# The products over partitions of a stick-breaking attention kept in a PSUM bank, and the results of the feed-forward's inner units put first

## The chip, the cores and the metric

The kernel runs on one core of a Trainium2 chip. A core has a matrix engine (PE), a vector engine (DVE), a scalar engine (ACT), a general engine (POOL) and a queue engine (SP) that mostly starts transfers. Each works through its own instructions in a fixed order and waits at semaphores for the others. SBUF is the working memory; PSUM holds eight banks of 128 partitions by 512 float32, into which PE writes and which DVE and ACT can read and write. POOL touches SBUF alone. The metric is the time of one execution on the device, in microseconds, lower being better.

## The reference

One layer of a hybrid encoder over a sequence of 2048 positions with 1024 channels, in float32. After an RMS norm, one projection feeds three mixers; their results are joined, projected back and added, and a squared-ReLU feed-forward follows.

```python
h = _rmsnorm(x, g_attn); p = h @ w_in            # 2816 columns
y_a = a_b * causal_conv3(a_c * a_h)
g = causal_conv31(b0 * sigmoid(b1)) + b_conv_b   # 256 channels
y_b = silu(_layernorm(g, ln_b_g, ln_b_b))
# y_c: stick-breaking attention, 8 heads of 64
z = q @ k.T * scale
log_beta = log_sigmoid(z)
log_1m = where(s < t, log_beta - z, 0)
suffix = reverse_cumsum(log_1m) - log_1m
a = where(s < t, exp(log_beta + suffix), 0)
o = a @ v
x = x + concat([y_a, y_b, y_c]) @ w_out
h2 = _rmsnorm(x, g_ffn)
x = x + square(relu(h2 @ w_ff1)) @ w_ff2         # 4096 inner units
return _rmsnorm(x, g_final)
```

The attention has no softmax: the weight of key s for query t is sigmoid(z) there, times the product of sigmoid(-z) over all keys between s and t. That running product over keys is what the changed code works out.

## The kernel before

Activations lie transposed, channels on partitions and 512 positions along a row, so the sequence makes four blocks (tb 0 to 3). Each float32 product is computed as three matmuls over a high and a low half of the operands (`mm3`, lines 103, 105 and 107, which is why most PE instructions carry these lines). The splitting into halves is `split` (L88 on ACT, L90 on DVE or POOL).

**Two large stages.** In the first, `p_half(0)` and `p_half(1)` compute the input projection of two blocks each. Beside them run the convolution mixer (`mixer_b`), the splitting of weights, and, in the second half, the attention of the first block. In the second stage, `block(tb)` computes for each of the four blocks the output projection, the 32 inner units `ffn1(c)` and, for each group of four of them, the second product `ffn2(g)`; beside blocks 0 to 2 runs the attention of blocks 1 to 3.

**The order of the work.** Work that runs beside the main line is a Python generator that yields a cost now and then. `weave(main, sides)` advances each side in proportion to the main line: an entry `(side, cost, t0, t1, last)` means that the side has come through `cost` units when the main line goes from t0 to t1. This gives the program order. A planner then simulates the engines with a cost model and writes each engine's instructions down in the order in which they came up there; among those that are ready it takes the earlier in program order, and what stands in `tc.high_priority(offset=HP)` is taken as 200 instructions earlier. On the chip each engine keeps this written order: if the next one has to wait, all behind it on that engine wait too.

**PSUM banks** are shared out by tags. In the second stage: three for the projections (`d`, also of the inner units `ps_u` and results `ps_y`), three for logits (`z`), one each for `ps_q` and `ps_o`. In the first stage: three `d`, one `c` for the convolution mixer, two `z`, one each for `q` and `o`.

**The attention** of one head and block. `a_pass1` (L542) makes logits per group of keys (`a_z`: matmuls L518 and L519 into a `z` bank), then two sigmoids on ACT: sigmoid(z) goes to the tile `A`, sigmoid(-z) to `om` (three diagonal groups, `a_diag`, L532 and L533) or back into the bank (L600). DVE multiplies up sigmoid(-z) over the groups in a tile `R` (L603), POOL multiplies `A` by it (L601). Keys are dealt out so that each partition holds a run of keys; what is left is the product over partitions. For this, DVE turns blocks of 32 by 32 around (L564 and L581 for the diagonal, 256 columns each, L609 for earlier keys, 512 columns) into a tile `T` of 16 segments of 33. Column 32 of each segment is set to 0 by POOL (L563, L608). `a_cross_a` (L612) then runs a scan backwards over the 528 columns (L617), where the tile `d1` (0, and 1 at each segment's end) restarts the product. Four groups of 32 partitions remain; their products go through a small tile `C` of 128 by 16 in SBUF: the last quarter is set to 1 (POOL, L620) or copied from `tot` (L622), three small multiplies go from quarter to quarter (L625), for the diagonal a fourth makes `tot` (L629), and one multiply applies `C` to `T` (L631). `a_pass2` turns the result back into the bank `ps_q` (L649), multiplies the `A` tiles by it (L652, L659), splits them (L88 on ACT and L90 on POOL, `Ahi` and `Alo`) and multiplies with the values (L697, L705, L706 into `ps_o`). With 8 heads and 4 blocks there are 32 products of the diagonal kind and 24 of the other, 56 in all.

**The feed-forward.** `ffn1(c)` runs 24 matmuls into a bank `ps_u`, then ACT squares the positive part in place (L917, L918) and copies it as the high half `fh` (L926), and DVE makes the low half `fl` (L927). `ffn2` runs 12 matmuls per output tile into `ps_y`, and DVE adds them to `acc` (L952). Since the norm's factor comes after the squaring, `acc` is multiplied by `ms` after the third inner unit: a small matmul spreads it into a `z` bank (L973, `spread`, L134), ACT copies it to SBUF, DVE multiplies the eight tiles (L975).

**The convolution mixer** (`mixer_b`, L441): per block and half of the channels 31 taps on DVE (L450, L452) into the bank `ps_c`, a copy by ACT (L456), a mean over channels on PE (L459), squares on ACT (L464), their sum on POOL (L467) and a column sum on PE (L127), a root on POOL (L118), and the normalised output.

Of the kernel before, what the change touches and what calls it, by code (L numbers as in the profile page):

```python
# [7 lines left out]
F32 = mybir.dt.float32  # L8
# [7 lines left out]
P = 128  # L16
# [18 lines left out]
def f(ap):  # L35
    return ap.bitcast(F32)
# [32 lines left out]
class Trunk:  # L69
# [126 lines left out]
    def attention_consts(self, ctx):  # L196
        nc = self.nc
        c = ctx.enter_context(self.tc.tile_pool(name="aconsts", bufs=1))
        self.d1 = c.tile([P, 16, 33], F32, name="d1")
        nc.vector.memset(self.d1, 0.0)  # L200
        nc.vector.memset(self.d1[:, :, 32:33], 1.0)
# [239 lines left out]
    def mixer_b(self, hf):  # L441
        nc = self.nc
        for tb in (2 * hf, 2 * hf + 1):
            acc = []
            for c in range(2):
# [10 lines left out]
                nc.scalar.activation(acc[c], t, AF.Copy)  # L456
            mean = self.psum("ps_mean", "c")
# [9 lines left out]
            nc.gpsimd.tensor_tensor(sqs[0], sqs[0], sqs[1], op=ALU.add)  # L467
            yv = self.rsqrt(self.colsum(sqs[:1], "c"), 1.0 / 256.0, LN_EPS)
# [73 lines left out]
    def a_pass1(self, g):  # L542
# [18 lines left out]
        nc.vector.tensor_tensor(om[:, hi2], om[:, lo], om[:, hi2], op=ALU.mult)  # L561
        T = pool.tile([P, 16, 33], F32, name="T", tag="T1", bufs=ab["T1"])
        nc.gpsimd.memset(T[:, :, 32:33], 0.0)  # L563
        nc.vector.transpose(T[:, 0:8, 0:32], om[:, hi2])  # L564
# [7 lines left out]
        R = new("R", ab["R"])  # L572
# [7 lines left out]
        nc.vector.tensor_tensor(om[:, hi2], om[:, hi2], R[:, hi2], op=ALU.mult)  # L580
        nc.vector.transpose(T[:, 8:16, 0:32], om[:, hi2])  # L581
        A0.append(t)
        yield 1
        tot = self.a_cross_a(g, T, None)
# [22 lines left out]
        T = pool.tile([P, 16, 33], F32, name="T", tag="T2", bufs=1)  # L607
        nc.gpsimd.memset(T[:, :, 32:33], 0.0)  # L608
        nc.vector.transpose(T[:, :, 0:32], R)  # L609
        self.a_cross_a(g, T, tot)  # L610

    def a_cross_a(self, g, T, seed):  # L612


        nc = self.nc
        fl = lambda x: x.rearrange("p a b -> p (a b)")[:, ::-1]
        nc.vector.tensor_tensor_scan(fl(T), fl(T), fl(self.d1), 1.0, op0=ALU.mult, op1=ALU.add)  # L617
        C = self.tiny.tile([P, 16], F32, name="C", tag="C", bufs=3)
        if seed is None:
            nc.gpsimd.memset(C[96:128], 1.0)  # L620
        else:
            nc.vector.tensor_copy(C[96:128], seed)  # L622
        for a in (2, 1, 0):
            s, d = slice(32 * a + 32, 32 * a + 64), slice(32 * a, 32 * a + 32)
            nc.vector.tensor_tensor(C[d], C[s], T[s, :, 0], op=ALU.mult)  # L625
        tot = None
        if seed is None:
            tot = self.tiny.tile([32, 16], F32, name="tot", tag="tot", bufs=2)
            nc.vector.tensor_tensor(tot, C[0:32], T[0:32, :, 0], op=ALU.mult)  # L629
        qt = T[:, :, 1:33]  # L630
        nc.vector.tensor_tensor(qt, qt, C.unsqueeze(2).to_broadcast([P, 16, 32]), op=ALU.mult)  # L631
        g["qd" if seed is None else "ql"] = qt
        return tot
# [190 lines left out]
    def block(self, tb, before):  # L824
# [76 lines left out]
        def ffn1(*cs):  # L901
# [14 lines left out]
            for c, ps in zip(cs, pus):  # L916
                nc.scalar.activation(ps, ps, AF.Relu)  # L917
                nc.scalar.activation(ps, ps, AF.Square)  # L918
                if tb == 3 and c > FC - G:

                    hi = self.at.tile([P, TB], F32R, name="fh", tag="Ahi", bufs=self.ab["Ahi"])
                    lo = self.at.tile([P, TB], F32R, name="fl", tag="Alo", bufs=self.ab["Alo"])
                else:
                    hi = hp.tile([P, TB], F32R, name="fh", tag="fh", bufs=G + 1)
                    lo = hp.tile([P, TB], F32R, name="fl", tag="fl", bufs=G + 1)
                nc.scalar.activation(hi, ps, AF.Copy)  # L926
                nc.vector.tensor_tensor(lo, ps, f(hi), op=ALU.subtract)  # L927
                fh[c], fl[c] = hi, lo
            yield 2.6 * len(cs)

        def ffn2(g, cols=slice(0, TB), ahead=0, again=0):
# [13 lines left out]
            for d in range(DC):  # L945
# [6 lines left out]
                nc.vector.tensor_tensor(acc[d][:, cols], acc[d][:, cols], ps, op=ALU.add)  # L952
# [19 lines left out]
        ms = hp.tile([P, TB], F32, name="ms", tag="ss", bufs=2)  # L972
        nc.scalar.activation(ms, self.spread(mt, "z"), AF.Copy)  # L973
        for d in range(DC):
            nc.vector.tensor_tensor(acc[d], acc[d], ms, op=ALU.mult)  # L975
        ss2 = hp.tile([P, TB], F32, name="ss2", tag="ss", bufs=2)
        sq7 = []
        for c in range(3, FC):
            yield from ffn1(c)
            if c < w2b:  # L980
                need2(c)
            if c % G == 0 and not (tb == 3 and c == FC - G):
                yield from ffn2(c // G - 1)
# [41 lines left out]
    def build(self):  # L1025
        tc = self.tc
        with ExitStack() as ctx:
# [6 lines left out]
            with ExitStack() as c1:  # L1034
# [12 lines left out]
                self.ab = dict(Kl=1, A0=6, om=2, R=1, T1=2, Alo=2, Ahi=2, Vl=1, late=1, yc=2)  # L1047
                weave(self.p_half(0), [(Side(self.mixer_b(0)), 83, 20, 225, True), (Side(self.x_norms()), 24, 60, 180, True)])
                self.heads = {}
                a0 = Side(self.attention([(h, 0) for h in range(H)]))  # L1050
                weave(self.p_half(1), [(Side(self.mixer_b(1)), 98, 0, 200, True), (a0, 28, 0, 210, True), (Side(self.pre_split()), len(self.presplit), 0, 200, True)])
            with ExitStack() as c2:
# [7 lines left out]
                self.ab = dict(Kl=1, A0=15, om=2, R=2, T1=1, Alo=3, Ahi=3, Vl=2, late=2, yc=1)  # L1060
# [59 lines left out]
```

## Time and profile before

| | |
|---|---|
| median of 3 runs | 2449.74 us (2442.66 to 2449.86) |
| the profiled execution | 2452.1 us, of which 2450.4 us are its span |
| mean granted PE clock | 0.992 of full speed |
| busy: PE, weight load | 2390.6, 2012.8 us |
| busy: DVE, ACT, POOL | 1620.1, 1040.6, 1161.3 us |
| DMA | 549.06 MB, 224 GB/s over the span |

The median is taken over runs without the profiler; the profile is of one further execution, and every duration below is of that one. "Busy" is the time in which an engine had at least one instruction under way. A row of a group names line, engine, operation, output and inputs, the shapes and the count; then the group's busy time and the mean of one instruction. A row of the waits says that an instruction stood because of another's: time in total, how often, the longest. A row of the windows gives, for a stretch of time, its length and then the busy time of PE, weight load, DVE, ACT and POOL, each with the number of instructions, then the granted clock of PE as a share of full speed, the DMA engines' busy share and GB/s.

### The profile page before, as it was taken

The page shows a single profiled execution, that of the slowest core. Times are in us where ns is not written, and L with a number is a line of the kernel's source. Part 1 is how long each engine was busy: PE and PEld are TensorE (multiplying, and loading weights), DVE is VectorE, ACT ScalarE, POOL GpSimd, SP SyncE. Part 2 cuts the span into 40 slices and gives each one's busy share as a digit, 9 for nine tenths or more (in the row PEclk, how much of TensorE's full clock was granted, in tenths as well). Part 3 has the DMA queues.
Part 4 walks back from the last instruction along what each step waited for, and adds up shares of the span by engine and source line. Part 5 has one row for each costly group of instructions (what it writes and reads, how often), then busy time and mean ns, then how long its engine had stood idle before and what let it go on. Part 6 is the DMA issues. An engine that isn't in the chain of part 4 may idle for free.

```text
span 2450.4 us, 32556 instructions
## 1 busy us (share of the span) xinstructions
PE 2390.6 (98%) x11316; PEld 2012.8 (82%) x11316; DVE 1620.1 (66%) x2380; ACT 1040.6 (42%) x1910; POOL 1161.3 (47%) x1221
## 2 busy tenths in 40 slices
PE   8999998999899999998999999999999999999998
PEld 7889877898788878887888888888888888888887
DVE  7957799943898977857777778577667735212114
ACT  5232532333466556534555555345555532121121
POOL 0342577641676666524676666168878720000000
PEclk9999999999999999999999999999999999999999
DMA  7569976779688777786877776876666556655555
GB/s 260 192 244 350 300 247 219 243 258 273 166 232 238 215 220 199 198 287 225 239 253 230 230 217 213 273 219 186 196 188 190 184 180 209 238 194 188 200 182 190
DMA packets 237061, 549.06 MB, mean 224 GB/s; under 512 B 26720, under 2 KB 100448, under 8 KB 218464
## 3 DMA queue, kind: packets, MB, share of 16 engines
q1 hardware_dynamic: 180304, 480.89, 58.1%
q0 software_dynamic: 37504, 56.64, 10.9%
q10 hardware_dynamic: 19088, 9.44, 1.3%
q8 instruction: 90, 1.47, 0.2%
q14 instruction: 75, 0.61, 0.1%
HBM read 390.38 MB, written 148.11 MB: 220 GB/s over the span
## 4 chain that ended last, share of the span: by engine, by line
PE 76%; DVE 15%; DMA 5%; issue 2%; POOL 1%; ACT 1%; SPq 0%; DVEq 0%; POOLq 0%; ACTq 0%
PE ps_y L107 8%; PE ps_y L103 8%; PE ps_y L105 8%; PE ps_u L103 7%; PE ps_u L105 7%; PE ps_u L107 7%; PE ps_p L105 4%; PE ps_p L107 4%; PE ps_p L103 4%; DVE A L659 2%; PE ps_x L103 2%; PE ps_z L518 2%; PE ps_x L105 2%; PE ps_x L107 2%; PE ps_z L519 2%
## 5 line engine op out<-in xcount | busy, mean ns | idle before, releaser
L90 POOL TENSOR_TENSOR Alo<-A,Ahi 128x512 fp32r<-128x512 f32 x288 | 395.1, 1383 | 104.2 <-PE ps_o L706 52.3
L952 DVE TENSOR_TENSOR acc<-acc,ps_y 128x512 f32<-128x512 f32 (+1 forms) x264 | 175.4, 667 | 195.6 <-PE ps_y L107 193.9
L107 PE MATMUL ps_y<-fl,w 128*128 128x512 f32 (+1 forms) x1056 | 279.8, 385 | 14.7 <-DVE fl L927 14.7
L103 PE MATMUL ps_u<-hh,w 128*128 128x512 f32 x1024 | 279.0, 393 | 6.2 <-DMA w<-s_w 6.2
L103 PE MATMUL ps_y<-fh,w 128*128 128x512 f32 (+1 forms) x1056 | 281.4, 386 | 2.5 <-DVE acc L952 1.3
L105 PE MATMUL ps_y<-fh,w 128*128 128x512 f32 (+1 forms) x1056 | 278.9, 384 | 0.0
L105 PE MATMUL ps_u<-hh,w 128*128 128x512 f32 x1024 | 275.0, 390 | 0.6 <-DVE w L90 0.6
L107 PE MATMUL ps_u<-hl,w 128*128 128x512 f32 x1024 | 275.0, 389 | 0.0
L601 POOL TENSOR_TENSOR A<-A,R 128x512 f32<-128x512 f32 x168 | 227.7, 1357 | 76.7 <-ACT A L599 54.6
L118 POOL TENSOR_TENSOR rs_y<-rs_v,mhalf 128x4 f32<-128x4 f32 (+1 forms) x13 | 14.7, 1131 | 523.3 <-DVE rs_v L117 486.1
L107 PEld LDWEIGHTS ps_y<-fl,w 128*128 128x128 f32 x1056 | 195.8, 189 | 55.9 <-DVE fl L927 17.0
L917 ACT ACTIVATE ps_u<-ps_u 128x512 f32<-128x512 f32 x128 | 74.8, 585 | 378.8 <-PE ps_u L107 378.5
L105 PEld LDWEIGHTS ps_y<-fh,w 128*128 128x128 f32 x1056 | 196.0, 189 | 40.2 <-DMA w<-wraw 0.4
L103 PEld LDWEIGHTS ps_y<-fh,w 128*128 128x128 f32 x1056 | 194.3, 189 | 40.7 <-DVE acc L952 2.1
L88 ACT ACTIVATE Ahi<-A 128x512 fp32r<-128x512 f32 x288 | 177.3, 627 | 118.4 <-PE ps_o L705 58.0
L105 PEld LDWEIGHTS ps_u<-hh,w 128*128 128x128 f32 x1024 | 192.1, 188 | 42.4 <-DVE w L90 1.5
L107 PEld LDWEIGHTS ps_u<-hl,w 128*128 128x128 f32 x1024 | 192.1, 188 | 40.1
L927 DVE TENSOR_TENSOR fl<-ps_u,fh 128x512 fp32r<-128x512 f32 x128 | 87.5, 685 | 207.1 <-ACT fh L926 206.6
L103 PEld LDWEIGHTS ps_u<-hh,w 128*128 128x128 f32 x1024 | 187.4, 189 | 42.5 <-DMA w<-s_w 6.4
L603 DVE TENSOR_TENSOR R<-ps_z,R 128x512 f32<-128x512 f32 x168 | 115.6, 688 | 126.4 <-ACT ps_z L600 93.8
L452 DVE SCALAR_TENSOR_TENSOR ps_c<-g,wb,ps_c 128x512 f32<-128x512 f32 x240 | 179.6, 748 | 4.6
L90 DVE TENSOR_TENSOR w<-wraw,w 128x512 fp32r<-128x512 f32 x152 | 150.4, 1007 | 24.1 <-ACT w L88 23.8
(175 smaller groups left out, 4881.2 us busy)
## 6 DMA issues: line engine op xcount, KB each, us to landing
w<-s_w SPq DMA_DIRECT2D x200, 512.0 KB, 3.4
w<-s_w SPq DMA_DIRECT2D x68, 1024.0 KB, 4.8
wraw<-in_w SPq DMA_DIRECT2D x192, 256.0 KB, 4.7
w<-s_w_out SPq DMA_DIRECT2D x64, 512.0 KB, 5.0
s_w<-w SPq DMA_DIRECT2D x32, 1024.0 KB, 5.4
s_w<-w SPq DMA_DIRECT2D x56, 512.0 KB, 4.4
Qd<-KQ SPq DMA_DIRECT2D x64, 256.0 KB, 6.4
xraw<-in_xT SPq DMA_DIRECT2D x48, 256.0 KB, 5.0
```

The costliest lines, as they stand in the source:

```text
L88: nc.scalar.activation(hi, x, AF.Copy)
L90: e.tensor_tensor(lo, x, f(hi), op=ALU.subtract)
L103: self.nc.tensor.matmul(ps, wh, xh, start=start and k == 0, stop=False)
L105: self.nc.tensor.matmul(ps, wl, xh, start=False, stop=False)
L107: self.nc.tensor.matmul(ps, wh, xl, start=False, stop=stop and k == n - 1)
L452: nc.vector.scalar_tensor_tensor(t, g[:, k : k + TB], self.wb[:, c, k : k + 1], t, op0=ALU.mult, op1=ALU.add)
L518: nc.tensor.matmul(z[:, oc], keys, g["qh"][:, qc], start=k == 0, stop=False)
L601: nc.gpsimd.tensor_tensor(t, t, R, op=ALU.mult)
L603: nc.vector.tensor_tensor(Rn, z, R, op=ALU.mult)
L917: nc.scalar.activation(ps, ps, AF.Relu)
L927: nc.vector.tensor_tensor(lo, ps, f(hi), op=ALU.subtract)
L952: nc.vector.tensor_tensor(acc[d][:, cols], acc[d][:, cols], ps, op=ALU.add)
```

## The change

The 32x32 turns of a head go into a bank of the tag `z` instead of into `T`; for that the diagonal's two halves are first collected in one tile `Rd` (a third user of the tag `R`, now with 2 buffers in both stages). The scan reads this bank and `d1`, without the extra column: `max` with `d1` (1 at each segment's end, 0 elsewhere) takes the place of the multiply-and-add that restarted it. `C` lies in the first 16 columns of the same bank, once the scan has read them. The two memsets are DVE's now: the last quarter of `C`, and a column of ones in `T` after the small multiplies. `T1` has one buffer in both stages.

`ms` stays in the bank that `spread` wrote, without ACT's copy; four of the eight multiplies come before the inner unit 3, four after it. The four instructions behind each inner unit, and the addition in `ffn2`, are put at high priority. `mixer_b` gets five more yields per block (three ahead of the mean, two ahead of the column sum), and its costs in `weave` become 115 (from 83) and 116 (from 98).

```diff
-        self.d1 = c.tile([P, 16, 33], F32, name="d1")
+        self.d1 = c.tile([P, TB], F32, name="d1")
         nc.vector.memset(self.d1, 0.0)
-        nc.vector.memset(self.d1[:, :, 32:33], 1.0)
+        nc.vector.memset(self.d1[:, 31:TB:32], 1.0)
...
                 nc.scalar.activation(acc[c], t, AF.Copy)
+            for _ in range(3):
+                yield 1.8
             mean = self.psum("ps_mean", "c")
...
             nc.gpsimd.tensor_tensor(sqs[0], sqs[0], sqs[1], op=ALU.add)
+            for _ in range(2):
+                yield 1.8
             yv = self.rsqrt(self.colsum(sqs[:1], "c"), 1.0 / 256.0, LN_EPS)
...
-        nc.vector.tensor_tensor(om[:, hi2], om[:, lo], om[:, hi2], op=ALU.mult)
-        T = pool.tile([P, 16, 33], F32, name="T", tag="T1", bufs=ab["T1"])
-        nc.gpsimd.memset(T[:, :, 32:33], 0.0)
-        nc.vector.transpose(T[:, 0:8, 0:32], om[:, hi2])
+        Rd = new("R", 2)
+        nc.vector.tensor_tensor(Rd[:, lo], om[:, lo], om[:, hi2], op=ALU.mult)
...
-        nc.vector.tensor_tensor(om[:, hi2], om[:, hi2], R[:, hi2], op=ALU.mult)
-        nc.vector.transpose(T[:, 8:16, 0:32], om[:, hi2])
+        nc.vector.tensor_tensor(Rd[:, hi2], om[:, hi2], R[:, hi2], op=ALU.mult)
...
-        T = pool.tile([P, 16, 33], F32, name="T", tag="T2", bufs=1)
-        nc.gpsimd.memset(T[:, :, 32:33], 0.0)
-        nc.vector.transpose(T[:, :, 0:32], R)
-        self.a_cross_a(g, T, tot)
+        self.a_cross_a(g, R, tot)
...
+        X = self.ps.tile([P, TB], F32, name="ps_t", tag="z", bufs=self.banks["z"])
+        T = self.at.tile([P, TB + 1], F32, name="T", tag="T1" if seed is None else "T2", bufs=1)
+        nc.vector.transpose(X, R)
-        nc.vector.tensor_tensor_scan(fl(T), fl(T), fl(self.d1), 1.0, op0=ALU.mult, op1=ALU.add)
-        C = self.tiny.tile([P, 16], F32, name="C", tag="C", bufs=3)
+        nc.vector.tensor_tensor_scan(T[:, 0:TB][:, ::-1], self.d1[:, ::-1], X[:, ::-1], 1.0, op0=ALU.max, op1=ALU.mult)
+        C = X[:, 0:16]
         if seed is None:
-            nc.gpsimd.memset(C[96:128], 1.0)
+            nc.vector.memset(C[96:128], 1.0)
...
+        first = T[:, 0:TB:32]
-            nc.vector.tensor_tensor(C[d], C[s], T[s, :, 0], op=ALU.mult)
+            nc.vector.tensor_tensor(C[d], C[s], first[s], op=ALU.mult)
...
-        qt = T[:, :, 1:33]
-        nc.vector.tensor_tensor(qt, qt, C.unsqueeze(2).to_broadcast([P, 16, 32]), op=ALU.mult)
+        nc.vector.memset(T[:, 32 : TB + 1 : 32], 1.0)
+        qt = T[:, 1 : TB + 1]
+        q3 = qt.rearrange("p (a b) -> p a b", a=16)
+        nc.vector.tensor_tensor(q3, q3, C.unsqueeze(2).to_broadcast([P, 16, 32]), op=ALU.mult)
...
-            for c, ps in zip(cs, pus):
-                nc.scalar.activation(ps, ps, AF.Relu)
...
+            with self.tc.high_priority(offset=HP):
+                for c, ps in zip(cs, pus):
+                    nc.scalar.activation(ps, ps, AF.Relu)
...
-                nc.vector.tensor_tensor(acc[d][:, cols], acc[d][:, cols], ps, op=ALU.add)
+                with self.tc.high_priority(offset=HP):
+                    nc.vector.tensor_tensor(acc[d][:, cols], acc[d][:, cols], ps, op=ALU.add)
...
-        ms = hp.tile([P, TB], F32, name="ms", tag="ss", bufs=2)
-        nc.scalar.activation(ms, self.spread(mt, "z"), AF.Copy)
+        ms = self.spread(mt, "z")
         for d in range(DC):
+            if d == DC // 2:
+                yield from ffn1(3)
             nc.vector.tensor_tensor(acc[d], acc[d], ms, op=ALU.mult)
...
-        for c in range(3, FC):
+        for c in range(4, FC):
...
-                weave(self.p_half(0), [(Side(self.mixer_b(0)), 83, 20, 225, True), (Side(self.x_norms()), 24, 60, 180, True)])
+                weave(self.p_half(0), [(Side(self.mixer_b(0)), 115, 20, 225, True), (Side(self.x_norms()), 24, 60, 180, True)])
...
-                weave(self.p_half(1), [(Side(self.mixer_b(1)), 98, 0, 200, True), (a0, 28, 0, 210, True), (Side(self.pre_split()), len(self.presplit), 0, 200, True)])
+                weave(self.p_half(1), [(Side(self.mixer_b(1)), 116, 0, 200, True), (a0, 28, 0, 210, True), (Side(self.pre_split()), len(self.presplit), 0, 200, True)])
```

More of the change, by code (lines that the diff above doesn't have):

```diff
@@ L571, in a_pass1 @@
         nc.gpsimd.tensor_tensor(t[:, hi2], t[:, hi2], om[:, lo], op=ALU.mult)
-        R = new("R", ab["R"])
+        R = new("R", 2)
         nc.vector.tensor_tensor(R[:, lo], om[:, lo], om[:, hi2], op=ALU.mult)
@@ L579, in a_pass1 @@
         nc.gpsimd.tensor_tensor(t, t, R, op=ALU.mult)
[L580 to L581 removed]
+        nc.vector.tensor_tensor(Rd[:, hi2], om[:, hi2], R[:, hi2], op=ALU.mult)
         A0.append(t)
         yield 1
[L584 removed]
+        tot = self.a_cross_a(g, Rd, None)
         if not i:
@@ L1059, in build @@
                 self.kmax = 1536
-                self.ab = dict(Kl=1, A0=15, om=2, R=2, T1=1, Alo=3, Ahi=3, Vl=2, late=2, yc=1)
+                self.ab = dict(Kl=1, A0=15, om=2, Alo=3, Ahi=3, Vl=2, late=2, yc=1)
                 at = Side(self.attention([(h, i) for i in (1, 2, 3) for h in range(H)]))
```

27 lines of the change are left out of this document (13 added, 14 removed).

## The prediction

> **What bounds the kernel now.** I read the page first, for the busy shares of the engines:
>
> ```profile
> span 2450.4 us, 32556 instructions
> ...
> PE 2390.6 (98%) x11316; PEld 2012.8 (82%) x11316; DVE 1620.1 (66%) x2380; ACT 1040.6 (42%) x1910; POOL 1161.3 (47%) x1221
> ```
>
> PE is busy for 2390.6 of 2450.4 us, and the change takes no matmul away. So it can only shorten PE's idle time, 59.8 us, and what PE loses where it runs slowly. The second view is therefore the waits of PE alone, longest first (engine, tile, line, what it waited for; total us, times, longest us):
>
> ```profile
> PE ps_y L107 <- DVE fl L927: 14.7, 6, 7.4
> PE ps_p L311 <- ACT wh L88: 6.5, 1, 6.5
> PE ps_u L103 <- DMA w<-s_w: 6.2, 6, 1.8
> PE ps_z L518 <- ACT A L533: 5.9, 1, 5.9
> PE ps_mean L459 <- ACT cb L456: 4.1, 1, 4.1
> PE ps_ss L127 <- POOL sq L467: 3.1, 1, 3.1
> PE ps_o L697 <- POOL Alo L90: 2.4, 2, 1.9
> PE ps_z L518 <- DVE R L603: 1.7, 2, 1.1
> PE ps_y L103 <- DVE acc L952: 1.3, 2, 1.0
> ```
>
> A few single waits make up most of it. The third view, windows of 10 us behind these waits, shows a second price (length; PE, weight load, DVE, ACT, POOL busy; then PE's granted clock, DMA share, GB/s):
>
> ```profile
> 380.00:390.00 10.00, 10.00 (x42) 7.96 (x41) 9.79 (x11) 1.26 (x2) 6.85 (x8) 0.85 0.93 362
> 390.00:400.00 10.00, 6.93 (x22) 5.52 (x21) 7.93 (x12) 3.83 (x8) 9.98 (x10) 0.66 0.46 136
> 640.00:650.00 10.00, 3.80 (x10) 3.05 (x11) 9.91 (x16) 1.09 (x2) 3.81 (x7) 0.66 0.41 118
> 860.00:870.00 10.00, 8.35 (x28) 6.94 (x29) 7.55 (x12) 2.59 (x6) 5.55 (x7) 0.66 0.36 110
> 1110.00:1120.00 10.00, 4.12 (x12) 2.80 (x11) 9.90 (x11) 4.32 (x9) 7.06 (x9) 0.67 0.71 240
> ```
>
> A granted clock of 0.66 over 10 us is 3.4 us lost. Every wait of 3 us or more inside the run is followed by such a loss, so it costs about double. DVE is nearly full in most of these rows. The timeline (start, length) shows what it did ahead of the longest:
>
> ```profile
> 632.08 12.27 DVE L975 TENSOR_TENSOR acc<-acc,ms 128x512 f32<-128x512 f32 x8
> ...
> 645.47 0.68 DVE L927 TENSOR_TENSOR fl<-ps_u,fh 128x512 fp32r<-128x512 f32 x1
> ```
>
> Eight multiplies by `ms` took 12.27 us, and the low half `fl` that PE needed stood behind them until 645.47. Ahead of the wait near 860, ACT was held too (in brackets its idle time and what ended it):
>
> ```profile
> 857.94 0.60 ACT L532 ACTIVATE om<-ps_z 128x512 f32<-128x512 f32 x1 [2.82 <-DVE T L564]
> ```
>
> **The change part by part: the products.** Why did DVE need so long? The instructions that use `T`, with shortest, median and longest duration in ns:
>
> ```profile
> L625 DVE TENSOR_TENSOR C<-C,T x168: 172/181/4320, 291.7 to 1960.0; 32x16 f32<-32x16 f32 x168
> L617 DVE TENSOR_TENSOR_SCAN T<-T,d x56: 1236/1644/5677, 289.6 to 1955.5; 128x528 f32<-128x528 f32 x56
> L631 DVE TENSOR_TENSOR T<-T,C x56: 671/674/1124, 295.4 to 1960.3; 128x512 f32<-128x512 f32 x56
> L649 DVE STREAM_TRANSPOSE ps_q<-T x56: 704/709/727, 297.3 to 1961.0; 128x512 f32<-128x512 f32 x56
> L564 DVE STREAM_TRANSPOSE T<-om x32: 396/433/447, 273.1 to 1913.3; 128x256 f32<-128x256 f32 x32
> L581 DVE STREAM_TRANSPOSE T<-om x32: 427/445/447, 288.6 to 1915.5; 128x256 f32<-128x256 f32 x32
> ```
>
> A multiply of 32x16 takes 172 ns at best and 4320 at worst. The rows with two inputs in SBUF stretch, L617 and L625 by microseconds and L631 by up to 0.45 us; the turns (L649, L564, L581), with one input, do not. The groups (busy us, mean ns) show the same beside a multiply that reads PSUM, L603:
>
> ```profile
> L452 DVE SCALAR_TENSOR_TENSOR ps_c<-g,wb,ps_c 128x512 f32<-128x512 f32 x240 | 179.6, 748 | 4.6
> ...
> L603 DVE TENSOR_TENSOR R<-ps_z,R 128x512 f32<-128x512 f32 x168 | 115.6, 688 | 126.4 <-ACT ps_z L600 93.8 <-issue 14.3 <-POOL A L601 13.3
> L617 DVE TENSOR_TENSOR_SCAN T<-T,d 128x528 f32<-128x528 f32 x56 | 101.9, 1819 | 1.1
> L625 DVE TENSOR_TENSOR C<-C,T 32x16 f32<-32x16 f32 x168 | 90.0, 536 | 5.6
> ...
> L975 DVE TENSOR_TENSOR acc<-acc,ms 128x512 f32<-128x512 f32 x32 | 33.4, 1109 | 2.6 <-ACT ms L973 2.6
> ```
>
> The change puts one input of L617, L625, L631 and L975 into PSUM. For the scan the floor is 1.236 us times 512/528, 1.20 us, the ceiling today's mean of 1.82; I take 1.20, since L603 at 0.688 shows no surcharge for a bank over L631 at 0.674. So 56 x (1.82 - 1.20) = 35 us of DVE go. The small multiplies: between 0.18 and today's 0.536; I take 0.2, 168 x 0.34 = 56 us. `ms`: 32 x (1.109 - 0.688) = 13 us, and ACT's four copies go, for which DVE waited 2.6 us. The turns: 32 x (0.433 + 0.445 - 0.709) = 5 us. DVE gains two memsets, nearest to this row (same shape, stepped):
>
> ```profile
> L201 DVE MEMSET d<- 128x16 f32 x1 | 0.1, 72 | 0.1
> ```
>
> That is (32 + 56) x 0.072 = 6 us, at most. DVE's sum: 1620 - 35 - 56 - 13 - 5 + 6 = about 1517 us busy. None of this is time of the kernel by itself; it counts where PE waits for DVE.
>
> One rule speaks against `ms` in its bank. The Trainium skill, "VectorE: DVE Perf Modes", section "Rules for kernel authors", advises to copy a matmul's output from PSUM to SBUF first if many operations will use it. By it the eight multiplies would rather get dearer. The rows L603 and L975 disagree: 688 ns from PSUM, 1109 ns on average from SBUF; at best they are equal.
>
> POOL loses 56 + 32 memsets, and with them the waits in its queue (who waited for the instructions on `T`: us, times):
>
> ```profile
>   POOL T L608: 54.2, 22
>   POOL T L563: 45.1, 21
>   ACT om L532: 28.5, 6
> ```
>
> POOL stood 99.3 us with its split `Alo` queued behind, which PE's `ps_o` needs; I count nothing for that, though the 2.4 us row could go. `om` is free one turn earlier, since `Rd` takes its product out; that shortens ACT's 28.5 us.
>
> **What PE gets back**, by edit. High priority puts L917 to L927 ahead of attention work in the written order; no DMA is moved past anything by it. That, with the shorter DVE queue, removes the `fl` waits: 14.7 us, and 3.4 us of clock at 640 and at 860, 21.5 us. What is late next there is `fh` on ACT, ready at about 635 in the first case, two us ahead of PE's need. `ms` from its bank, four and four: the wait for ACT's A at 1110, 5.9 us plus 3.3 us of clock, 9.2 us; DVE was held in it just as at 632. Behind the added inner unit only its weights are asked for, in the same order as before. The yields in `mixer_b`: the mean's 4.1 us, the column sum's 3.1 us, clock 1.5 and 3.4 us, 12.1 us; the three steps, 5.4 of 116 units spread over 200 us, move the matmul 9 us later, the two steps 6 us, more than each wait. L952 at high priority: 1.3 us. Together 44.1 us. Not touched: the first load's 6.5 us, the weight DMAs' 6.2 us, the 1.7 us for R.
>
> At the column sum the wait was only 3.1 us. The Trainium skill, "TensorE: Matmul & The Clock Gate", section "HAM oscillation — how this bites in real kernels", has the rule that idle gaps above about 3.4 us cost clock. By it that wait would have been free of the second price, and the sum 40.7 us. The row 390 to 400 at 0.66 decides for 44.1.
>
> **What it adds for PE.** `X` holds one of three `z` banks (one of two in the first stage) from the turn to the last multiply: 0.709 + 1.20 + 3 x 0.2 + 0.15 + 0.674, 3.3 us if nothing comes between, 56 times; `ms` holds one through a whole inner unit, four times. The next logits on PE wait for that bank, and PE's queue, the feed-forward's matmuls too, stands behind them. DVE's turn itself waits for a free bank, with `fl`, R and `acc` behind it; `Rd` and R now fill both buffers of their tag, so ACT's first R of the earlier keys (L597) waits until POOL and DVE are done with them, with the squarings behind it. No row shows this. The nearest rows from below: L603 releases a `z` bank 168 times and PE lost 1.7 us to it, 0.01 us each. From above: an event like the one at 1110, 9.2 us, at every eighth `X`, 64 us. I take two new events of 3.5 us and 3.4 us of clock, about 14 us: near the lower end, because L603 is the same kind of release, but not nothing, since the planner writes the whole order anew.
>
> The sum on the profiled execution: 2452.1 - 44.1 + 14 = 2422.0 us. That execution lies 2.4 us above the median of the three runs, so 2419.6, rounded to **2420 us**.
>
> **The rivals.**
>
> Half 1 becomes DVE's. Its load there (same columns as the windows above):
>
> ```profile
> 270.00:520.00 250.00, 238.60 (x1153) 199.32 (x1152) 222.43 (x325) 86.67 (x160) 186.14 (x201) 0.97 0.78 255
> ```
>
> DVE is busy 222 of 250 us and full near 390. The 62 taps of a block (62 x 0.748 = 46 us of DVE) were spread over 36/98 of 200 us, 73 us; now 36/116, 62 us: 12 points more load just where the projection's results are taken out. For it: the row 380 to 390. Against it: PE hardly waits for those results now, and the yields leave DVE freer in between. Then the mixer's 12.1 us stay and one more event comes: 44.1 - 12.1 - 14 - 7 = 11 us of gain, 2439 us.
>
> The time stays where it is. The waits are put down to an engine by which semaphore came last; if what stretches is only moved (L580, L578, L573, L561 and the weight split keep two SBUF inputs), the new order makes six events of 7 us elsewhere, 42 us, and about 2450 us results. That is also what comes if the bank doesn't free the scan and the small multiplies from their stretching.
>
> Slower: the `z` banks. The same place as the cost above, at its upper end: 64 us lost, 44.1 won, 2452.1 + 20 - 2.4 = 2470 us. It decides from 44.1/9.2, that is from five such events among 56 products. For it: the wait at 1110 is just this kind, PE's order standing behind a `z` bank. Against it: the stretching that made that event is what the change removes.
>
> Better than forecast: no new event, and the `Alo` wait gone: 2452.1 - 44.1 - 2.4 - 2.4 = 2403 us.
>
> **How the numbers follow.** Forecast (2405 to 2432 us) 0.54; half 1 bound by DVE (2432 to 2442) 0.14; better (below 2405) 0.04; no net change (2442 to 2457) 0.14; slower by the banks (above 2457) 0.14. About 0.3%, 7 us, is what a measurement of this kernel can tell from no change. So faster 0.72, same 0.14, slower 0.14. The range from 2402 to 2453 us takes in the forecast, the first rival, the full gain and most of the unchanged case; it leaves out the slower case and the rest, about 2 in 10.
>
> **What would show it.** In the profile after: L625 and the scan with medians near their minima and no durations of several us, DVE near 1517 us busy; no wait of PE for `fl` above 2 us, none at the mean and the column sum; granted clock at 1.00 from 600 to 1200 us. The forecast is wrong if PE's waits show a `z` matmul behind `X`'s multiply, DVE turns waiting for a bank, or L597 waiting for R; if DVE gets its 100 us and PE's idle time stays near 60 us; or if half-clock windows come back at new places.

## The result and the profile after

The changed kernel takes **2420.49 us** (median of 5 runs, 2415.74 to 2422.02) against 2449.74 us (median of 5, 2442.66 to 2455.13): a ratio of 0.9875, 95% interval 0.9852 to 0.9897. The forecast was 2420. Its profiled execution took 2415.74 us and was the shortest of the five, so the two profiles lie further apart than the medians do, 36.4 us of span against 29.3 us. First its page, the shares of the engines:

```profile
span 2414.0 us, 32476 instructions
...
PE 2379.1 (99%) x11316; PEld 2005.3 (83%) x11316; DVE 1534.0 (64%) x2436; ACT 1043.6 (43%) x1906; POOL 1128.6 (47%) x1133
```

The span is 36.4 us shorter with the same matmuls. PE's idle time fell from 59.8 to 34.9 us, its busy time by 11.5 us; most of that is clock: on work, stretches at half clock cost 13.0 us before and 4.0 us after. DVE lost 86 us where 103 were forecast. Second, PE's waits, the longest first:

```profile
PE ps_p L311 <- ACT wh L88: 6.2, 1, 6.2
PE ps_u L103 <- DMA w<-s_w: 6.1, 6, 1.6
PE ps_z L522 <- DVE T L635: 4.8, 3, 3.4
PE ps_R L134 <- POOL rs_y L118: 2.8, 2, 1.7
PE ps_z L522 <- ACT A L537: 2.7, 1, 2.7
```

The waits for `fl`, at the column sum and for `Alo` are gone, and the mean's, in a row further down, is 0.4 us. New is the third row: a logits matmul that waits for the multiply by `C`, the last reader of `X`. Third, the windows around it and at the places where the clock had been at 0.66:

```profile
320.00:330.00 10.00, 6.65 (x26) 5.30 (x25) 9.77 (x21) 3.27 (x7) 3.35 (x4) 0.83 0.79 288
360.00:370.00 10.00, 7.32 (x30) 5.72 (x29) 9.67 (x16) 2.23 (x4) 6.77 (x7) 0.88 0.88 288
...
640.00:650.00 10.00, 10.00 (x48) 8.34 (x47) 7.74 (x13) 6.80 (x14) 10.00 (x13) 1.00 0.48 115
860.00:870.00 10.00, 10.00 (x46) 8.23 (x45) 4.61 (x8) 5.29 (x10) 5.50 (x6) 1.00 0.81 166
1110.00:1120.00 10.00, 10.00 (x46) 8.49 (x45) 5.90 (x9) 5.72 (x11) 4.72 (x4) 1.00 0.46 165
```

In this execution the second stage holds its full clock. The two losses left stand behind the two waits of logits in the first stage, 1.7 us each (the second low stretch goes on past 370; from 365 to 373 the clock is 0.79). It is not so in every execution: a further kernel with the same written order, `no_hp` below, shows a clock of 0.66 from 1086 to 1091, from 1096 to 1101 and from 2065 to 2070. Fourth, the instructions on the bank `X`, which the trace calls `ps_t` (ns: shortest, median, longest):

```profile
L627 DVE TENSOR_TENSOR ps_t<-ps_t,T x168: 173/181/194, 293.5 to 1922.3; 32x16 f32<-32x16 f32 x168
L616 DVE STREAM_TRANSPOSE ps_t<-R x56: 710/727/729, 288.8 to 1918.9; 128x512 f32<-128x512 f32 x56
L618 DVE TENSOR_TENSOR_SCAN T<-d,ps_t x56: 1194/1212/1222, 290.1 to 1920.4; 128x512 f32<-128x512 f32 x56
L635 DVE TENSOR_TENSOR T<-T,ps_t x56: 672/689/693, 298.0 to 1922.6; 128x512 f32<-128x512 f32 x56
```

None of these instructions stretches any more: the small multiplies end at 194 ns at worst, before at 4320, the scan at 1222, before at 5677.

Where the time went, by stretches that hold the same work. Each begins with the first logits matmul (the second half of the projection) or with the first output-projection matmul of a block. Before:

```profile
268.90:557.40 288.50, 277.10 (x1473) 237.78 (x1473) 234.44 (x346) 99.09 (x183) 190.40 (x205) 0.98 0.77 252
557.40:1038.80 481.40, 467.22 (x2140) 388.86 (x2139) 386.70 (x542) 270.93 (x503) 287.66 (x328) 0.99 0.76 217
1038.80:1536.20 497.40, 485.71 (x2218) 408.33 (x2218) 376.60 (x547) 257.48 (x475) 297.44 (x309) 0.99 0.75 237
1536.20:2039.20 503.00, 497.67 (x2254) 417.56 (x2253) 318.55 (x472) 241.47 (x439) 311.26 (x308) 1.00 0.64 199
```

After:

```profile
270.10:553.10 283.00, 273.00 (x1458) 233.48 (x1457) 228.47 (x352) 96.15 (x180) 179.22 (x188) 0.99 0.79 257
553.10:1018.30 465.20, 462.85 (x2139) 385.67 (x2139) 359.89 (x561) 272.49 (x502) 280.74 (x297) 1.00 0.78 225
1018.30:1508.00 489.70, 484.37 (x2218) 407.07 (x2217) 344.62 (x563) 258.40 (x474) 286.71 (x285) 1.00 0.76 241
1508.00:2003.40 495.40, 494.61 (x2254) 417.41 (x2253) 295.94 (x486) 242.65 (x438) 303.72 (x292) 1.00 0.66 202
```

Second half of the projection: 5.5 us shorter. Block 0: 16.2. Block 1: 7.7. Block 2: 7.6. The first half and block 3 together hardly changed. These are differences of one profile each; a table behind the experiments shows which of them come again.

### The profile page after: what moved, and what is told of

Same layout as the page of the kernel before. It is cut to its first block, busy times and chain, and to the rows that moved or that the text cites. A ratio compares the mean times of both kernels' runs of the same rounds, so it can differ in the third digit from the quotient of the medians.

```text
span 2414.0 us, 32476 instructions
## 1 busy us (share of the span) xinstructions
PE 2379.1 (99%) x11316; PEld 2005.3 (83%) x11316; DVE 1534.0 (64%) x2436; ACT 1043.6 (43%) x1906; POOL 1128.6 (47%) x1133
## 4 chain that ended last, share of the span: by engine, by line
PE 84%; DMA 6%; DVE 6%; issue 1%; ACT 1%; POOL 1%; SPq 1%; POOLq 0%; DVEq 0%; ACTq 0%
PE ps_y L107 9%; PE ps_y L105 9%; PE ps_y L103 9%; PE ps_u L103 9%; PE ps_u L105 9%; PE ps_u L107 9%; PE ps_p L107 4%; PE ps_p L105 4%; PE ps_p L103 3%; PE ps_z L522 2%; PE ps_z L523 2%; PE ps_x L103 2%; PE ps_x L105 2%; PE ps_x L107 2%; PE ps_o L710 2%; PE ps_o L709 2%
## 5 line engine op out<-in xcount | busy, mean ns | idle before, releaser
L90 POOL TENSOR_TENSOR Alo<-A,Ahi 128x512 fp32r<-128x512 f32 x288 | 385.3, 1347 | 147.0 <-ACT Ahi L88 69.9
L103 PE MATMUL ps_u<-hh,w 128*128 128x512 f32 x1024 | 279.4, 392 | 6.4 <-DMA w<-s_w 6.1
L103 PE MATMUL ps_y<-fh,w 128*128 128x512 f32 (+1 forms) x1056 | 281.2, 384 | 0.0
L602 POOL TENSOR_TENSOR A<-A,R 128x512 f32<-128x512 f32 x168 | 222.4, 1326 | 121.7 <-ACT A L600 103.3
L107 PE MATMUL ps_y<-fl,w 128*128 128x512 f32 (+1 forms) x1056 | 278.6, 383 | 0.1
L107 PE MATMUL ps_u<-hl,w 128*128 128x512 f32 x1024 | 275.8, 390 | 0.0
L107 PEld LDWEIGHTS ps_y<-fl,w 128*128 128x128 f32 x1056 | 195.0, 188 | 39.4 <-DVE fl L932 0.6
L107 PEld LDWEIGHTS ps_u<-hl,w 128*128 128x128 f32 x1024 | 192.1, 188 | 40.1
L103 PEld LDWEIGHTS ps_y<-fh,w 128*128 128x128 f32 x1056 | 193.6, 188 | 36.8
L103 PEld LDWEIGHTS ps_u<-hh,w 128*128 128x128 f32 x1024 | 186.9, 188 | 42.4 <-DMA w<-s_w 8.1
```

What stands on the lines that cost most here:

```text
L90: e.tensor_tensor(lo, x, f(hi), op=ALU.subtract)
L103: self.nc.tensor.matmul(ps, wh, xh, start=start and k == 0, stop=False)
L107: self.nc.tensor.matmul(ps, wh, xl, start=False, stop=stop and k == n - 1)
L602: nc.gpsimd.tensor_tensor(t, t, R, op=ALU.mult)
```

## The experiments

Twelve kernels, in three sets of four. Each set has its own runs of the kernel before beside it; only ratios to those are compared. The first set leaves out one part of the change, the second makes one part alone, the third takes parts asunder.

### Leaving out high priority

```diff
-            with self.tc.high_priority(offset=HP):
-                for c, ps in zip(cs, pus):
-                    nc.scalar.activation(ps, ps, AF.Relu)
+            for c, ps in zip(cs, pus):
+                nc.scalar.activation(ps, ps, AF.Relu)
...
-                with self.tc.high_priority(offset=HP):
-                    nc.vector.tensor_tensor(acc[d][:, cols], acc[d][:, cols], ps, op=ALU.add)
+                nc.vector.tensor_tensor(acc[d][:, cols], acc[d][:, cols], ps, op=ALU.add)
```

> The changed kernel without high priority for the four instructions behind an inner unit and for the addition in ffn2; all else changed. The changed kernel took 2420.5 us, the one before 2449.7. Theory: the written order made the low half fl late, so waits of PE for fl come back, at least two of over 3 us with the half clock behind them: 2430 to 2442 us. Rival: what made fl late was the stretching of DVE's instructions, which the bank has removed: 2418 to 2424 us and no wait for fl above 2 us.

2423.28 us, ratio 0.9884 (0.9864 to 0.9904). The rival held: PE's waits hold one row for `fl`, of 0.2 us. The reason is plain in the written order: compared engine by engine, with tile numbers left out, this kernel and the changed one have the same instructions in the same order on PE, DVE, ACT, POOL and SP. In company of the other parts the edit does nothing, and the 0.0009 between the two ratios is what the same order gives twice.

### Leaving out the bank for the products

```diff
-        Rd = new("R", 2)
-        nc.vector.tensor_tensor(Rd[:, lo], om[:, lo], om[:, hi2], op=ALU.mult)
+        nc.vector.tensor_tensor(om[:, hi2], om[:, lo], om[:, hi2], op=ALU.mult)
+        T = pool.tile([P, 16, 33], F32, name="T", tag="T1", bufs=ab["T1"])
+        nc.gpsimd.memset(T[:, :, 32:33], 0.0)
+        nc.vector.transpose(T[:, 0:8, 0:32], om[:, hi2])
...
```

> The changed kernel with the products over partitions worked out in SBUF as before (T of 16 segments of 33, C in SBUF, POOL's memsets); high priority, ms in its bank and the yields stay. Theory: DVE's stretching is back (DVE busy about 1600 us, the small multiplies at a mean of 0.5 us), but fl and acc are first in the order, so PE loses only through late sigmoids and logits: 2424 to 2434 us. Rival 1: the bank is most of the gain: 2438 to 2450 us. Rival 2: the order is all that counted, and the banks' new waits in the first stage (about 10 us with clock) go with them: 2408 to 2416 us.

2435.59 us, ratio 0.9937 (0.992 to 0.9954). That lies between the theory and rival 1: the bank is worth about half of the gain beside the rest. DVE is busy 1609.4 us again, and among PE's longest waits are now these, where the projection's results are taken out, at the mean and at `fl` (total us, times, longest):

```profile
PE ps_p L103 <- DVE u L355: 5.4, 1, 5.4
PE ps_mean L461 <- ACT cb L456: 5.0, 1, 5.0
PE ps_y L107 <- DVE fl L932: 4.8, 6, 1.4
```

The mean waits for 5.0 us although the yields are there. The `fl` waits are short without the bank too, so `ms` in its bank is enough to shorten them.

### Leaving out ms in its bank

```diff
-        ms = self.spread(mt, "z")
+        ms = hp.tile([P, TB], F32, name="ms", tag="ss", bufs=2)
+        nc.scalar.activation(ms, self.spread(mt, "z"), AF.Copy)
         for d in range(DC):
-            if d == DC // 2:
-                yield from ffn1(3)
             nc.vector.tensor_tensor(acc[d], acc[d], ms, op=ALU.mult)
```

> The changed kernel with ms copied to SBUF by ACT and all eight multiplies at one place, as before. Theory: the multiplies stretch to over 8 us in the first blocks again (mean of one about 1.1 us against 0.69), and logits or fl behind them make PE wait once or twice with the half clock: 2426 to 2434 us. Rival: with fl ahead by priority nothing on PE waits for them: 2418 to 2423 us.

2423.51 us, ratio 0.9882 (0.9866 to 0.9897): within the interval of the whole change. The multiplies do stretch again (mean 1.044 us), but PE has no wait for `fl` in its rows. The time lies just above the rival's 2418 to 2423, and the rival's reason fell: priority moves nothing beside the other parts. The bank for the products is enough as well. Near 628 the eight multiplies take 6.87 us here, against 12.27 in the kernel before, and the `fl` behind them is done at 636.4, before PE needs it.

### Leaving out the yields

```diff
-            for _ in range(3):
-                yield 1.8
...
-            for _ in range(2):
-                yield 1.8
```

and the costs 83 and 98 as before.

> The changed kernel with the convolution mixer's yields and its costs (83, 98) as before. Theory: PE waits again for the mean (about 4 us) and the column sum (about 3 us) with the half clock behind them, 12 us: 2430 to 2435 us. Rival: those waits came from a DVE that was late by its stretching, which the bank has eased, and the slower taps even help in the first stage: 2412 to 2421 us.

2427.24 us, ratio 0.9898 (0.9881 to 0.9914). Between the two. The wait for the mean is 2.2 us, that at the column sum is not among the longer ones, and a wait of logits behind a sigmoid, 4.8 us, takes their place. By the medians the yields are worth 3 to 6 us beside the rest (0.9898 against the 0.9875 and 0.9884 of one written order); these intervals overlap. Two more things speak for them. The kernel with the bank alone, below, gave 0.9927 (0.9909 to 0.9946); it differs from the one without `ms`, 0.9882 (0.9866 to 0.9897), in the yields and the priority; that is 11 us, and those intervals do not overlap. And the second half of the projection takes 281.8 to 283.0 us in the changed kernel, in the one without priority and in the one without `ms`, but 288.2 and 289.2 in the two that have the bank and no yields; the stretch ahead of it is only some 1 to 2 us longer.

### One part alone

The four parts are the same edits, each made alone on the kernel before.

> The kernel before with the products over partitions in a z bank alone. Theory (the parts stand in for one another: each would remove the fl waits by itself): DVE's stretching at the small multiplies and the scan goes, the fl wait near 860 (8 us with clock) and small waits go, but the eight multiplies by ms from SBUF still hold fl near 640 and the logits near 1110 (20 us), the mixer's waits stay in part, and X adds 5 us in the first stage: ratio 0.995 to 0.998. Rival (the parts add up, as leaving out one gave 0.9937 for the rest): 0.993 to 0.995.

2430.68 us, ratio 0.9927 (0.9909 to 0.9946): just better than the rival's range, and the theory fell. Alone, the bank for the products gives 18 us, and its waits of PE hold no row for `fl`.

> The kernel before with high priority behind the inner units and for the addition in ffn2 alone. Theory (the parts stand in for one another): the fl waits with their clock, some 21 us, go, the wait near 1110 and the mixer's stay: ratio 0.990 to 0.994. Rival (the parts add up; without it the changed kernel lost 3 us): 0.998 to 1.000.

2448.14 us, ratio 0.9997 (0.9981 to 1.0013): nothing, and the theory fell. The longest wait for `fl` is still 7.5 us. Its timeline there:

```profile
635.26 12.27 DVE L977 TENSOR_TENSOR acc<-acc,ms 128x512 f32<-128x512 f32 x8
...
648.66 0.68 DVE L928 TENSOR_TENSOR fl<-ps_u,fh 128x512 fp32r<-128x512 f32 x1
```

The eight multiplies take their 12.27 us and `fl` stands behind them as before. The written orders are the same on PE, ACT, POOL and SP; DVE's differs at six places, the first of them its 2001st instruction of 2380, near 1805 us. A likely reason, which no run shows, is that the planner's cost model does not count the stretching: then `fl` was never late in its reckoning, and a priority that chooses among ready instructions had almost nothing to choose.

> The kernel before with ms in its bank and the multiplies four and four alone. Theory (stand in for one another): the multiplies cost 0.69 us each in every block, the fl wait near 640 (11 us with clock) and the logits' wait near 1110 (9 us) go, the fl wait near 860 and the mixer's stay: ratio 0.990 to 0.994. Rival (the parts add up; without it the changed kernel lost 3 us): 0.998 to 1.000.

2438.11 us, ratio 0.9959 (0.9945 to 0.9973): faster, by 10 us, less than the theory said and more than the rival. The longest wait for `fl` is 1.4 us in its profile, and the row of logits that wait for ACT's `A` is down to 0.5 us. Only the first counts as a cure. In the kernel with high priority alone that second row is 0.4 us as well, though its order is that of the kernel before until 1805 (PE had waited 3.3 us for weights just ahead there): the wait near 1110 doesn't come in every execution. The multiplies now (busy us, mean ns):

```profile
L976 DVE TENSOR_TENSOR acc<-acc,ps_R 128x512 f32<-128x512 f32 x32 | 19.5, 679 | 1.3 <-PE ps_R L134 1.3
```

> The kernel before with the convolution mixer's yields and costs alone. Theory (as predicted): the waits for the mean and the column sum with their clock, 12 us, go and nothing else changes: ratio 0.994 to 0.996. Rival (the parts add up; without it the changed kernel lost 6 us): 0.997 to 0.998.

2450.08 us, ratio 0.9996 (0.998 to 1.0011): no change shown, and the interval leaves room for a gain of 5 us at most. Its waits show the column sum's gone, but the mean's at 3.5 us and a new one of 3.7 us for a result of the projection (L355). The predicted 12 us were not there to be had by moving these matmuls alone.

### C alone back in SBUF

```diff
-        C = X[:, 0:16]
+        C = self.tiny.tile([P, 16], F32, name="C", tag="C", bufs=3)
```

> The changed kernel with C alone in SBUF again (128 by 16; the scan still reads the bank). The small multiplies then have two inputs in SBUF. Theory (an instruction stretches when both inputs are in SBUF and POOL is at work): the small multiplies' mean goes from 0.18 to about 0.4 to 0.5 us, the scan's stays at 1.21, DVE busy rises by some 40 to 60 us, and the time by 3 to 8 us, ratio 0.989 to 0.991. Rival (the gain came from the new order, or from POOL's memsets going): the mean stays below 0.25 us, ratio 0.987 to 0.988.

2440.69 us, ratio 0.9956 (0.9941 to 0.9971): the mechanism as expected, its price far above. In the groups of DVE (busy us, mean ns) the small multiplies stretch again and the scan, which still reads the bank, does not:

```profile
L618 DVE TENSOR_TENSOR_SCAN T<-d,ps_t 128x512 f32<-128x512 f32 x56 | 67.9, 1212 | 0.9
...
L627 DVE TENSOR_TENSOR C<-C,T 32x16 f32<-32x16 f32 x168 | 94.4, 562 | 5.6
```

DVE is busy 1605.0 us, 71 more than after. But the time rose by 20 us, some two thirds of the whole gain. Two things come together here: the stretching, and a written order that differs on every engine, because this tile frees the bank at another point. PE's longest wait is now this one:

```profile
PE ps_z L522 <- DVE T L618: 11.8, 4, 6.1
```

Logits wait for the scan, the bank's last reader, which DVE reaches late. How much of the 20 us is stretching and how much order isn't settled by this run.

### X in another bank in the first stage

```diff
-        X = self.ps.tile([P, TB], F32, name="ps_t", tag="z", bufs=self.banks["z"])
+        X = self.ps.tile([P, TB], F32, name="ps_t", tag=self.xtag, bufs=self.banks[self.xtag])
```

with `xtag` "q" in the first stage and "z" in the second.

> The changed kernel with X in the bank of ps_q instead of a z bank in the first stage; that bank is read and written by DVE alone. Theory (the charge for X is paid in the first stage, where PE's logits stand behind it: 4.8 us for the multiply by C, 2.7 us behind the sigmoids, 3.4 us of clock): these waits go, the first stage is 5 to 11 us shorter, ratio 0.983 to 0.986. Rival (DVE is full there, and its lateness comes out at the next result that PE waits for): ratio 0.986 to 0.988.

2418.55 us, ratio 0.9864 (0.9842 to 0.9885). The stretch from the first logits to the first output projection takes 278.8 us where it took 283.0, and the wait for `X`'s multiply falls from 4.8 to 1.3 us. But PE now waits 3.8 us for ACT's `Ahi` and 2.4 us for the mean, as the rival said. The ratio lies in the rival's range, at its border to the theory, and inside the interval of the change: a gain isn't shown.

### The two edits at ms, each alone

The split of the eight multiplies, with `ms` still copied:

```diff
         for d in range(DC):
+            if d == DC // 2:
+                yield from ffn1(3)
             nc.vector.tensor_tensor(acc[d], acc[d], ms, op=ALU.mult)
```

> The kernel before with the multiplies by ms four and four around inner unit 3, ms still copied to SBUF. Theory (what hurts is two inputs in SBUF): the multiplies still stretch (mean about 1.0 us), but a shorter run of them stands before fl; half of the gain of both edits: ratio 0.997 to 0.999. Rival (the run of eight in one place is the harm, the place of ms is nothing): 0.995 to 0.997, as both edits gave 0.9959.

2448.91 us, ratio 0.999 (0.9975 to 1.0005): no change shown, and again for a plain reason. The written order is the same as before on all five engines; the eight multiplies stand where they were. The longest wait for `fl` is 7.3 us.

The bank, with the eight in one place:

```diff
-        ms = hp.tile([P, TB], F32, name="ms", tag="ss", bufs=2)
-        nc.scalar.activation(ms, self.spread(mt, "z"), AF.Copy)
+        ms = self.spread(mt, "z")
```

> The kernel before with ms left in its z bank, the eight multiplies in one place. Theory (what hurts is two inputs in SBUF): the multiplies take 0.69 us each in every block, 5.5 us in all, the fl wait near 640 falls below 2 us and the logits' wait near 1110 goes: ratio 0.995 to 0.997, as both edits gave 0.9959. Rival (the run of eight is the harm): fl still waits 3 us or more near 640, ratio 0.998 to 1.000.

2437.69 us, ratio 0.9945 (0.9924 to 0.9966): all that both edits gave (0.9959). The written order of this kernel and of the one with both edits is the same on all five engines. The mean of one multiply is 677 ns, the longest wait for `fl` 2.4 us, near 852. So it is the place of `ms` that counts, not the split.

**Which stretches come again.** Several of these kernels share a written order, so their profiles show what differs between executions. The four stretches are those of the windows above (us; kernels of one order stand in one row; the one with high priority alone shares its order until 1805 us):

| kernels | second half of the projection | block 0 | block 1 | block 2 |
|---|---|---|---|---|
| before, `ms_split`, `only_hp` | 288.5, 294.2, 291.9 | 481.4, 475.2, 479.3 | 497.4, 498.2, 491.4 | 503.0, 503.7, 503.3 |
| `only_ms`, `ms_bank` | 293.9, 289.3 | 468.1, 472.1 | 492.7, 490.8 | 502.3, 503.4 |
| `only_bank` | 289.2 | 473.0 | 492.7 | 495.4 |
| after, `no_hp` | 283.0, 282.0 | 465.2, 466.0 | 489.7, 494.8 | 495.4, 495.7 |

One order varies by up to 7 us in a stretch. In block 0, in block 2 and in the second half of the projection the first and the last row lie apart; in block 1 they overlap, so its 7.7 us are not shown. The gain of `ms` in its bank lies mostly in block 0, that of block 2 comes with the bank for the products.

## Why the prediction was right

**What bounds the kernel.** Right. PE's matmuls stayed, and what was won is idle time and clock. The two other limits feared did not come: in the second half of the projection DVE is busy 228.5 of 283.0 us (before 234.4 of 288.5), and the banks brought two events, not the seven of the slower case.

**Every wait "costs about double".** Too high. The price of the clock was read off windows of 10 us, and these take in the wait itself. From 638.8 to 646.2 PE stood, and the clock there is already 0.75; on the work behind it, from 646.2 to 649.3, it is 0.51, which loses 1.5 us and not 3.4. At 1110 the loss is 1.8 us and not 3.3. Over its five events the prediction booked 15.0 us of clock where some 11 were lost on work. Nor do all the events return: in `ms_split`, with the order of before, the longest wait for `fl` near 860 is 1.1 us, in `only_hp` there is none.

**The stretching of DVE.** Right in kind and nearly in size: scan 1.212 us (1.20 forecast), small multiplies 0.183 (0.2), `ms` 0.679 (0.688), memsets 0.072 each. DVE came to 1534.0 us and not to about 1517. Of the 17 us, 15 are in the four products over diagonal groups that keep two inputs in SBUF: before, the means of L561, L573, L578 and L580 sum to 0.648 + 0.844 + 0.923 + 1.095 = 3.51 us, after to

```profile
L580 DVE TENSOR_TENSOR R<-om,R 128x256 f32<-128x256 f32 x32 | 37.1, 1158 | 16.1 <-POOL om L541 16.0
L582 DVE TENSOR_TENSOR R<-om,R 128x256 f32<-128x256 f32 x32 | 33.0, 1032 | 0.8
...
L575 DVE TENSOR_TENSOR R<-om 128x256 f32<-128x256 f32 x32 | 30.3, 947 | 7.8 <-POOL om L541 7.8
L566 DVE TENSOR_TENSOR R<-om 128x256 f32<-128x256 f32 x32 | 27.0, 844 | 6.7 <-POOL om L541 6.7
```

0.844 + 0.947 + 1.158 + 1.032 = 3.98 us, 15 us more over 32 products. It looks as if a part of the stretching moved to those that still have it, as the rival of no net change feared; that cause is argued and not tested, and it is a small part, about a seventh of the 107 us that the scan, the small multiplies and `ms` shed.

**High priority removes the `fl` waits, 21.5 us.** The step that failed. The waits went, and not by priority: the same order comes out with it and without it beside the other parts, and alone it gives a ratio of 0.9997. The 7.4 us near 640 are removed by `ms` in its bank (in the kernels with that part alone the longest is 1.4 to 2.4 us), and by the bank for the products, which alone leaves no `fl` wait while the multiplies are in SBUF. Each cures it alone, so leaving out `ms` cost little. The forecast named "the shorter DVE queue" beside priority; that half was right. So the largest part by measurement, the 18 us of the bank alone, had no term of its own in the sum. Whether all of it comes from the stretching isn't shown: the bank changes the written order too, and no run has the one without the other.

**`ms` in its bank, 9.2 us.** Nearly right in size, 10 us alone, but partly by luck. The step priced the wait at 1110; the table has most of the gain in block 0, where `ms` removes the `fl` wait near 640 that was booked under priority. The split of the multiplies, which the step counted too, does nothing.

**The yields, 12.1 us.** Mis-sized. Alone they bring no gain that the runs show (0.9996), and 12 us lie outside the interval. PE's matmul stands later in the order, but the tap multiplies still end late, since DVE is full there; in the kernel without the bank the mean waits 5.0 us with the yields in place. Beside all the rest they bring 3 to 6 us, beside the bank without `ms` up to 11.

**The charge for new waits, 14 us.** Right in place and nearly in size: 4.8 us behind `X`'s multiply, 2.7 us behind a sigmoid, 3.4 us of clock, 10.9 in all, every one in the first stage with its two `z` banks. The timeline of the longest (start, length) shows why the 3.3 us of holding were not kept:

```profile
317.79 0.72 DVE L616 STREAM_TRANSPOSE ps_t<-R 128x512 f32<-128x512 f32 x1
318.42 0.71 DVE L452 SCALAR_TENSOR_TENSOR ps_c<-g,wb,ps_c 128x512 f32<-128x512 f32 x1
319.04 1.20 DVE L618 TENSOR_TENSOR_SCAN T<-d,ps_t 128x512 f32<-128x512 f32 x1
320.17 0.72 DVE L452 SCALAR_TENSOR_TENSOR ps_c<-g,wb,ps_c 128x512 f32<-128x512 f32 x1
...
324.69 0.68 DVE L635 TENSOR_TENSOR T<-T,ps_t 128x512 f32<-128x512 f32 x1
```

Taps of the convolution come between the steps, and `X` is held for 7.6 us. The waits for R's buffers came to 0.7 us of ACT.

**Not forecast.** Block 2 became 7.6 us shorter, though no wait of over 1.4 us was cured there. It is 495.4 us in the kernel with the bank alone, and 503.5 us where only the bank is missing. PE's idle time in it fell from 5.3 to 0.8 us: before, seven waits of 0.3 to 1.4 us, of which the sum had counted those of L107 for `fl` and of L103 for the addition L952, 2.1 us. PE's busy time fell by 3.1 us at the same clock; what did that stays open. **That the sum came out right is in part luck.** Priority had 22.8 us in it and gave nothing of its own, the clock was priced some 4 us too high, the yields gave about half of their 12 us. The bank for the products, for which the sum had a charge and no gain of its own, made up for it: the total was better than its parts.

The rule of the Trainium skill ("VectorE: DVE Perf Modes", "Rules for kernel authors") on copying from PSUM first was rightly set aside: `ms` read from its bank eight times costs 0.679 us each, and the bank gives 10 us. Its rule that only idle gaps above about 3.4 us cost clock ("TensorE: Matmul & The Clock Gate", "HAM oscillation — how this bites in real kernels") isn't borne out: behind the wait of 2.7 us the window from 360 stands at 0.88, and in `no_hp`, behind a wait of 1.8 us, the clock is 0.66 from 365 to 370.

## What to carry to other kernels

Where DVE's instructions vary many times in length while POOL is at work, look for those with two inputs in SBUF, the small ones too, and move one input into a PSUM bank that is free for the time; 168 multiplies of 32x16 cost this kernel 59 us of DVE more than they do from a bank. Before putting an edit down to the order of instructions, compare the written orders: two of the edits here, the split and (beside the other parts) the priority, left them as they were. Kernels that turn out to have one order also tell how far two executions of it lie apart. And when a sum is made from the longest waits, count the clock on the work alone, and remember that the short waits behind the same cause can go with them.

## What the runs showed of the hardware

A small instruction of DVE can lose to several of POOL's in a row. Before, the three multiplies of 32x16 by `C` ran like this on DVE:

```profile
380.89 5.65 DVE L625 TENSOR_TENSOR C<-C,T 32x16 f32<-32x16 f32 x3
```

and POOL at that time like this:

```profile
382.50 1.29 POOL L90 TENSOR_TENSOR Alo<-A,Ahi 128x512 fp32r<-128x512 f32 x1
383.74 1.29 POOL L350 TENSOR_TENSOR ac<-ac,R 128x512 f32<-128x512 f32 x1
384.99 1.29 POOL L579 TENSOR_TENSOR A<-A,R 128x512 f32<-128x512 f32 x1
```

5.65 us for some 0.6 us of work. The longest of the three, 4.32 us, begins at 382.01 and ends at 386.33, 0.05 us after POOL's third. The Trainium skill, "SBUF — State Buffer", sections "Who interferes with whom" and "SBUF: two separate sides", says that a DVE instruction with two SBUF inputs contends with a GpSimd instruction that reads SBUF, and that whoever starts first has the port for the whole instruction. The trace agrees that such pairs contend; that one waits out several in a row is more than the rule says. Where POOL has nothing to do, in the last block, the same eight multiplies by `ms` that took 12.27 us took under five:

```profile
2096.52 4.91 DVE L975 TENSOR_TENSOR acc<-acc,ms 128x512 f32<-128x512 f32 x8 [1.68 <-ACT ms L973]
```
